# The 62 steps of each inversion of 32-blocks moved to GpSimd, and low parts of projection weights moved to VectorE

## The chip, the cores and the metric

One core of one Trainium2 chip runs the whole kernel. The metric is the device time of one execution in microseconds, taken as the median of several runs. The core has a matrix engine (TensorE, PE in the profile), VectorE (DVE), ScalarE (ACT), GpSimd (POOL) and SyncE (SP), each with its own list of instructions that it works through in order; they wait for each other through semaphores. DMA transfers are issued from the lists of SP and POOL.

## The reference, cut to what matters

The model has two layers. Layer 0 mixes tokens with a bidirectional gated delta rule, layer 1 with neighbourhood attention; each is followed by a gated feed-forward block with a convolution. There are 128 context tokens and 512 latent tokens of width 1024. The change lies in layer 0, in the triangular solve of the delta rule:

```
decay = jnp.where(lower, jnp.exp(jnp.where(lower, diff, 0.0)), 0.0)
kb = kc * bc[..., None]
a_mat = jnp.where(strict, jnp.einsum('nbhid,nbhjd->nbhij', kb, kc) * decay, 0.0)
eye = jnp.broadcast_to(jnp.eye(C, dtype=f32), a_mat.shape)
t_mat = lax.linalg.triangular_solve(eye + a_mat, eye, left_side=True, lower=True)
u = jnp.einsum('nbhij,nbhjd->nbhid', t_mat, vc * bc[..., None])
w = jnp.einsum('nbhij,nbhjd->nbhid', t_mat, kb * jnp.exp(gc)[..., None])
```

and in the projections that feed it (`proj = h @ w_in`), where queries, keys, values and gates of 8 heads of width 128 are made. The state is then carried over the chunks, in both directions, and the outputs are normalised and gated.

## The kernel before

**Products.** All large products are in float32 split in two: a high part, which the matrix engine takes at its faster rate, and a low part, the rest. `pass3` (L385, L386, L387) issues three matmuls for each: high times high, the data's low part times the weight's high, the data's high times the weight's low. `weights` (L359) issues the load of a 128x1024 block of weights on SP; `split` casts the high part on ScalarE (L373) and subtracts for the low part on `lo or net.lo_engine` (L375). In the stage of layer 0's mixer `net.lo_engine` is GpSimd; it is VectorE again from the output product's weights on, whose first two blocks (`go0` 0 and 1) are still split inside the stage.

**The mixer.** The class `Gdn` (L580) works head by head. A table written out by hand, `SCHED` (L573), gives the order in which the steps are put to the program: `k`, `q`, `v`, `z` are projections of one head (a product of 640 columns in two halves, a short convolution on VectorE at L442, an activation); `K` makes the decay masks (`decay`, L692 to L708), the token-wise keys, the five diagonal blocks of 128x128 in both directions (`keys`: PE at L761, then ten operations on VectorE into M at L786) and sends 32-blocks of them to a scratch tensor `md` (L795, DMAs on SP; a transpose on VectorE, L791, comes between). `I` inverts the unit triangular 32-blocks of two heads at once (`invert`), `M` puts four inverted 32-blocks together to one of 128 (`merge`, PE at L848 with copies on ScalarE and VectorE, L865 and L869 and L884), `Q` and `V` prepare queries and values, `S` is the scan over the blocks (`scan`, L906 to L972), `F` normalises and multiplies with the gate (`finish`, from L974), `a` is a tile of the modulation.

**The inversion.** Two heads give 80 partitions, each with one 32x32 block. `invert` loads lN from `md` (L806, on SP), sets lY to the unit matrix with two memsets on GpSimd (L808, L809), and runs 31 steps of two instructions: an outer product lP of a column of lN and a row of lY (L813), and its addition into lY (L819). The instructions have 31 to 256 elements per partition, and each needs the one before. Then lY goes to the scratch `yd` (L820, SP), a copy on VectorE writes its transpose over lN (L821), and that goes to `wd` (L822, SP). lN, lY and lP have one buffer each, so one inversion follows another. There are four: I0 to I3 for heads 0 and 1, 2 and 3, 4 and 5, 6 and 7.

**The merge** loads its blocks from `yd` and `wd` by DMAs on SP (L834 to L841) and first clears two corners of W6 (L829, L830) on GpSimd; W6 has one buffer.

**What sets the order.** The program is written in the order of `SCHED`, and a scheduler then puts the instructions of each engine in a list by readiness under its own costs and by priority. `PR` raises the priority of some steps: scans by 2000, inversions by 1000, merges by 500, keys by 200. Once made, the list of an engine is fixed: an instruction whose input is late holds up all that stand behind it on that engine.

Of the kernel before, what the change touches and what calls it, by code (L numbers as in the profile page):

```python
# [15 lines left out]
ALU = mybir.AluOpType  # L16
# [15 lines left out]
HBLK = ((0, 1, 2), (3, 4))  # L32
HN = 384
NFT = 22
PR = {"S": 2000, "I": 1000, "M": 500, "K": 200}
WSTB = 2
EARLY = 4
UNITS = 6
# [39 lines left out]
def run(steps):  # L78
    while True:
        try:  # L80
            next(steps)
        except StopIteration as end:
            return end.value
# [496 lines left out]
class Gdn:  # L580
# [218 lines left out]
    def invert(self, nh, md, yd, wd, name):  # L799

        nc = self.nc
        L = nh * 40
        N = self.gp.tile([128, 32, 32], F32, tag="lN", name=f"lN{name}", bufs=1)
        Y = self.gp.tile([128, 32, 32], F32, tag="lY", name=f"lY{name}", bufs=1)
        P = self.gp.tile([128, 256], F32, tag="lP", name=f"lP{name}", bufs=1)
        nc.sync.dma_start(N[:L], md.rearrange("h q d b r c -> (h q d b) r c")[:L])  # L806
        Yf = Y.rearrange("p r c -> p (r c)")
        nc.gpsimd.memset(Yf[:L], 0.0)  # L808
        nc.gpsimd.memset(Yf[:L, 0:1024:33], 1.0)  # L809
        for i in range(31, 0, -1):  # L810
            n = 32 - i
            pr = P[:L, : i * n].rearrange("p (j c) -> p j c", c=n)
            nc.vector.tensor_tensor(  # L813
                pr,
                N[:L, :i, i : i + 1].to_broadcast([L, i, n]),
                Y[:L, i : i + 1, i:].to_broadcast([L, i, n]),
                ALU.mult,
            )
            nc.vector.tensor_tensor(Y[:L, :i, i:], Y[:L, :i, i:], pr, ALU.add)  # L819
        nc.sync.dma_start(yd.rearrange("h q d b r c -> (h q d b) r c")[:L], Y[:L])  # L820
        nc.vector.tensor_copy(N[:L].rearrange("p r c -> p c r"), Y[:L])  # L821
        nc.sync.dma_start(wd.rearrange("h q d b r c -> (h q d b) r c")[:L], N[:L])  # L822
# [200 lines left out]
    def run(self):  # L1023
        net, nc, dp = self.net, self.nc, self.dp
        scr = {}
        adas = [(0, m, t) for t in range(KT) for m in (2, 4) if m == 2 or t < 4]

        def step(op, h):
            if op == "k":
                self.kT[h] = self.proj(1, h)  # L1030
            elif op == "q":
                self.qT[h] = self.proj(0, h)
            elif op == "v":
                self.vT[h] = self.proj(2, h)
            elif op == "K":
                if h % 2 == 0:
                    scr[h // 2] = [
                        dp.tile([2, 4, 2, NBLK, 32, 32], F32, tag=t, name=f"{t}{h // 2}", bufs=2)
                        for t in ("md", "yd", "wd")
                    ]  # L1040
                self.decay(h)
                self.keys(h, scr[h // 2][0][h % 2])
            elif op == "I":
                self.invert(2, *scr[h], h)
            elif op == "Q":
                self.queries(h)
            elif op == "V":
                self.values(h)
            elif op == "M":
                self.merge(h, scr[h // 2][1][h % 2], scr[h // 2][2][h % 2])  # L1050
            elif op == "S":
                self.scan(h)
            elif op == "F":
                self.finish(h)
            elif op == "z":
                self.gate(h)
            elif op == "a":
                for _ in range(min(h, len(adas))):
                    net.ada_tile(*adas.pop(0), self.gp, 1)

        for t in SCHED.split():
            if t[0] in PR:
                with net.tc.high_priority(PR[t[0]]):
                    step(t[0], int(t[1]))
            else:
                step(t[0], int(t[1]))
        while adas:
            net.ada_tile(*adas.pop(0), self.gp, 1)
        net.scale_vec(0, 2)
        self.first = {m: net.weights(net.a["w_gout"][m], KT, f"go0{m}") for m in range(2)}  # L1070
        for half in (0, 1):
            for h in range(8):
                for hf, c0, c1, _ in SEGS:
                    if hf == half:
                        g = self.G[h][:, c0:c1]
                        hh = net.hh[:, h, c0:c1]
                        nc.scalar.copy(hh, g)
                        nc.vector.tensor_tensor(net.hl[:, h, c0:c1], g, hh.bitcast(F32), ALU.subtract)
# [564 lines left out]
```

## Time and profile before

| what | value |
| --- | --- |
| median of 3 runs | 1931.02 us (1923.04 to 1935.49) |
| profiled execution | 1937.65 us |
| its span | 1935.7 us |
| mean granted clock of TensorE | 0.97 |
| first and last step of the four inversions | 116.1 to 156.4, 165.0 to 215.2, 323.9 to 378.3, 456.7 to 508.1 us |
| mixer of layer 0 | to about 595 us |

Times inside the trace count from the start of its span. Each row of the timeline gives start, duration, engine, line, operation, output and inputs by their names in the program, and shapes; what stands in brackets is the time in which the engine stood idle just before, and the operation that ended the wait. A line such as L813 is the line of the kernel before; lines behind 1042 are one higher in the changed kernel. PEld is TensorE's loading of weights, which goes on beside its matmuls. The granted clock is the share of full speed at which TensorE was let run.

### The profile page before, as it was taken

Reading aid. Unit: us, or ns where it says so; the run is one execution under the profiler, and the core shown is the slowest. Engines: PE = TensorE matmul, PEld = TensorE weight load, DVE = VectorE, ACT = ScalarE, POOL = GpSimd, SP = SyncE. Lnnn points to the kernel's source line nnn. Section 1 sums busy time; section 2 is a strip of 40 time slices with the busy share of each in tenths; the row PEclk is TensorE's granted clock in tenths of the full one; section 3 lists DMA queues with packets and bytes.
Section 4 is the critical chain, followed back from the end, with each engine's and each line's share of the span. In section 5 each row is a group of like instructions: output and inputs, shape, how many; then the busy total and the mean of one; then the engine's idle time right before and its main releaser. Section 6 shows DMA issues by size and latency. Waiting matters only on the chain.

```text
span 1935.7 us, 34324 instructions
## 1 busy us (share of the span) xinstructions
PE 1839.9 (95%) x13587; PEld 1749.1 (90%) x13587; DVE 1278.4 (66%) x3100; ACT 724.3 (37%) x1456; POOL 263.0 (14%) x317
## 2 busy tenths in 40 slices
PE   6889998999988999999999999999999999999998
PEld 5878888887878999999999988888889999999998
DVE  6687657757655999865356689655678843553564
ACT  4453344343334432133134344444454431331343
POOL 1332123121201211210000121111131000000000
PEclk9889899998888999999999999999999999999999
DMA  7223133222204355543223155322233322222231
GB/s 289 72 80 105 37 103 112 89 52 88 60 22 144 111 169 166 169 152 103 62 77 112 54 166 159 91 77 69 66 127 102 122 69 73 84 77 70 82 97 55
DMA packets 102480, 194.15 MB, mean 100 GB/s; under 512 B 39496, under 2 KB 59034, under 8 KB 99560
## 3 DMA queue, kind: packets, MB, share of 16 engines
q1 hardware_dynamic: 94528, 165.50, 27.7%
q0 software_dynamic: 7248, 25.94, 4.3%
q8 instruction: 107, 1.75, 0.4%
q14 instruction: 53, 0.43, 0.1%
q10 hardware_dynamic: 544, 0.52, 0.1%
HBM read 183.09 MB, written 12.46 MB: 101 GB/s over the span
## 4 chain that ended last, share of the span: by engine, by line
PE 46%; DVE 5%; issue 2%; DMA 2%; ACT 1%; POOL 0%; DVEq 0%; POOLq 0%; ACTq 0%
PE duv L385 4%; PE duv L386 4%; PE duv L387 4%; PE dug L385 4%; PE dug L386 4%; PE dug L387 4%; PE rdn L385 4%; PE rdn L387 4%; PE rdn L386 4%; DMA adr<-w_adar 1%; PE no L1323 1%; DMA bias<-cols 1%; PE dvn L385 1%; PE s L1269 1%; PE dvn L387 1%
## 5 line engine op out<-in xcount | busy, mean ns | idle before, releaser
L385 PE MATMUL duv<-hh,whuv 128*128 128x256 f32 (+1 forms) x704 | 216.7, 308 | 5.4 <-DVE yv L442 5.4
L385 PE MATMUL rdn<-F,whdn 128*128 128x384 f32 (+1 forms) x704 | 216.6, 308 | 3.5 <-DVE X L451 3.5
L386 PE MATMUL duv<-hl,whuv 128*128 128x256 f32 (+1 forms) x704 | 216.2, 307 | 0.0
L385 PE MATMUL dug<-hh,whug 128*128 128x256 f32 (+1 forms) x704 | 215.4, 306 | 0.8 <-DVE yg L442 0.8
L387 PE MATMUL duv<-hh,wluv 128*128 128x256 f32 (+1 forms) x704 | 216.0, 307 | 0.0
L386 PE MATMUL rdn<-F,whdn 128*128 128x384 f32 (+1 forms) x704 | 216.0, 307 | 0.0
L387 PE MATMUL rdn<-F,wldn 128*128 128x384 f32 (+1 forms) x704 | 215.8, 306 | 0.0
L386 PE MATMUL dug<-hl,whug 128*128 128x256 f32 (+1 forms) x704 | 215.4, 306 | 0.0
L387 PE MATMUL dug<-hh,wlug 128*128 128x256 f32 (+1 forms) x704 | 215.4, 306 | 0.0
L385 PEld LDWEIGHTS duv<-hh,whuv 128*128 128x128 f32 x704 | 132.8, 189 | 6.0 <-ACT whug L373 3.5
L385 PEld LDWEIGHTS rdn<-F,whdn 128*128 128x128 f32 x704 | 132.6, 188 | 4.2 <-issue 2.3
L385 PEld LDWEIGHTS dug<-hh,whug 128*128 128x128 f32 x704 | 132.2, 188 | 1.0 <-issue 1.0
L387 PEld LDWEIGHTS duv<-hh,wluv 128*128 128x128 f32 x704 | 132.8, 189 | 0.0
L386 PEld LDWEIGHTS rdn<-F,whdn 128*128 128x128 f32 x704 | 132.7, 189 | 0.0
L387 PEld LDWEIGHTS rdn<-F,wldn 128*128 128x128 f32 x704 | 132.7, 189 | 0.0
L386 PEld LDWEIGHTS duv<-hl,whuv 128*128 128x128 f32 x704 | 132.6, 188 | 0.0
L387 PEld LDWEIGHTS dug<-hh,wlug 128*128 128x128 f32 x704 | 132.2, 188 | 0.0
L386 PEld LDWEIGHTS dug<-hl,whug 128*128 128x128 f32 x704 | 132.2, 188 | 0.0
L451 DVE SCALAR_TENSOR_TENSOR X<-rdn,mods,X 128x128 f32<-128x128 f32 (+1 forms) x144 | 54.9, 433 | 116.5 <-PE rdn L387 116.4
L373 ACT CAST whdn<-wstdn 128x896 fp32r<-128x896 f32 (+1 forms) x48 | 47.0, 979 | 214.1 <-PE rdn L386 122.0
L373 ACT CAST whug<-wstug 128x1024 fp32r<-128x1024 f32 x44 | 46.2, 1050 | 137.7 <-PE dug L386 114.5
L375 DVE TENSOR_TENSOR wldn<-wstdn,whdn 128x896 fp32r<-128x896 f32 (+1 forms) x48 | 54.3, 1132 | 60.6 <-ACT whdn L373 60.5
(701 smaller groups left out, 4909.3 us busy)
## 6 DMA issues: line engine op xcount, KB each, us to landing
wstuv<-w_up SPq DMA_DIRECT2D x44, 512.0 KB, 3.5
wstug<-w_up SPq DMA_DIRECT2D x44, 512.0 KB, 3.5
adat<-w_ada SPq DMA_DIRECT2D x20, 1024.0 KB, 5.7
adr<-w_adar POOLq DMA_DIRECT2D x80, 256.0 KB, 3.2
wstdn<-w_dn SPq DMA_DIRECT2D x32, 448.0 KB, 3.4
wstdn<-w_dn SPq DMA_DIRECT2D x16, 512.0 KB, 3.6
adr<-w_adar SPq DMA_DIRECT2D x32, 256.0 KB, 2.9
wstqT<-w_gin SPq DMA_DIRECT2D x8, 512.0 KB, 3.6
```

Of the source, the lines that this page charges most:

```text
L373: nc.scalar.copy(wh[:, c], st[:, c])
L375: ins = eng.tensor_tensor(wl[:, c], st[:, c], wh[:, c].bitcast(F32), ALU.subtract).ins
L385: nc.tensor.matmul(out, a, mh, start=first, stop=False)
L386: nc.tensor.matmul(out, a, ml, start=False, stop=False)
L387: ins = nc.tensor.matmul(out, b, mh, start=False, stop=last).ins
L451: nc.vector.scalar_tensor_tensor(x, ps[:, base + c0 : base + c1], self.mod(l, gi, m, v), x, ALU.mult, ALU.add)
L1269: nc.tensor.matmul(ss[e][:, o], qb[H[e]], kk[H[e]], start=True, stop=True, tile_position=(64 * e, 0))
L1323: nc.tensor.matmul(out, vw[:n, cb, j, H[e]], pt[:n, 2 * e + j], start=(j == 0), stop=False, tile_position=(0, 64 * e))
```

## The change

Three edits. Both instructions of a step of the inversion (L813, L819) are issued on GpSimd in place of VectorE; the load, the memsets, the final copy (L821) and the DMAs stay where they were. The added priority of the inversions goes from 1000 to 100. And once the first inversion has been put to the program, `net.lo_engine` is VectorE, so that low parts of weights that come behind it in `SCHED` are subtracted there.

```diff
-PR = {"S": 2000, "I": 1000, "M": 500, "K": 200}
+PR = {"S": 2000, "I": 100, "M": 500, "K": 200}
...
         for i in range(31, 0, -1):
             n = 32 - i
             pr = P[:L, : i * n].rearrange("p (j c) -> p j c", c=n)
-            nc.vector.tensor_tensor(
+            nc.gpsimd.tensor_tensor(
                 pr,
                 N[:L, :i, i : i + 1].to_broadcast([L, i, n]),
                 Y[:L, i : i + 1, i:].to_broadcast([L, i, n]),
                 ALU.mult,
             )
-            nc.vector.tensor_tensor(Y[:L, :i, i:], Y[:L, :i, i:], pr, ALU.add)
+            nc.gpsimd.tensor_tensor(Y[:L, :i, i:], Y[:L, :i, i:], pr, ALU.add)
...
             elif op == "I":
                 self.invert(2, *scr[h], h)
+                net.lo_engine = nc.vector
```

In the lists of the changed kernel 28 low parts of 128x1024 stand on VectorE that stood on GpSimd: of v0, q1, v2, the gates and all later projections, 26 in all, and of the first two output blocks. Those of k2, q0, k3 and v1 stay on GpSimd. Rows of the lists follow; a row gives line, operation, output and inputs (with buffer numbers), and shape.

VectorE before, while head 3's blocks M3 are made and the first inversion runs:

```order
L819 TENSOR_TENSOR lY0_1325<-lY0_1325,lP0_1326 80x8x24
L786 SCALAR_TENSOR_TENSOR M3_1303<-kk3p_1297,D3_1289,dec3_1244 128x128
L813 TENSOR_TENSOR lP0_1326<-lN0_1324,lY0_1325 80x175
L786 SCALAR_TENSOR_TENSOR M3_1303<-kk3s_1296,D3_1289,dec3_1244 128x128
L819 TENSOR_TENSOR lY0_1325<-lY0_1325,lP0_1326 80x7x25
```

VectorE in the change, at the same place (wlzs0 and wlzs1 are low parts of gate weights, D3 the factors of head 3):

```order
L375 TENSOR_TENSOR wlzs0_2415<-wstzs00_2412,whzs0_2414 128x1024
L442 SCALAR_TENSOR_TENSOR qT1_1642<-dqT11_1617,sm_61,qT1_1642 128x256
L821 COPY lN0_1324<-lY0_1325 80x32x32
L375 TENSOR_TENSOR wlzs1_2474<-wstzs10_2471,whzs1_2473 128x1024
L752 TENSOR_SCALAR k3ss_1278<-k3ss_1278 128x5
L775 RECIPROCAL rk23_1287<-k3ss_1278 128x5
L779 TENSOR_TENSOR D3_1289<-rk23_1287,beta_669 128x5 x2
L780 TENSOR_SCALAR D3_1289<-D3_1289 128x5
L781 TENSOR_TENSOR D3_1289<-D3_1289,edl_691 128x5
L780 TENSOR_SCALAR D3_1289<-D3_1289 128x5
L781 TENSOR_TENSOR D3_1289<-D3_1289,edl_691 128x5
L786 SCALAR_TENSOR_TENSOR M3_1303<-kk3p_1297,D3_1289,dec3_1244 128x128
```

The copy that ends the inversion, which stood behind M3 and the last step, now stands ahead of all of head 3's D and M.

VectorE in the change, in the scan of head 3 (vm, S and w are the scan's values of one block; dec4 belongs to head 4's queries):

```order
L929 TENSOR_SCALAR vm301_4042<-sb301_4035,D3_1289 128x128
L929 TENSOR_SCALAR vm314_4057<-sb314_4050,D3_1289 128x128
L821 COPY lN2_3608<-lY2_3609 80x32x32
L966 SCALAR_TENSOR_TENSOR S030_4047<-S03_4006,egl_690,sb301_4035 128x128
L898 TENSOR_TENSOR dec4_2810<-kq4s_3693,dec4_2810 128x512
L966 SCALAR_TENSOR_TENSOR S130_4062<-S13_4008,egl_690,sb314_4050 128x128
```

The copy of the third inversion stands between two operations of the scan. In the same way that of the second stands in head 1's scan, between the operations w and vm, and that of the fourth in head 5's, behind the first two vm.

SP in the change, where the second inversion's load stands (W61 is head 1's corner tile, adat021 a block of modulation weights, ns00 and ns01 head 0's final states):

```order
L836 DMA W61_2001<-wd0_720 32x5x32
L837 DMA W61_2001<-wd0_720 32x5x32
L838 DMA W61_2001<-yd0_719 32x5x32
L839 DMA W61_2001<-yd0_719 32x5x32
L795 DMA md1_1013<-MT3_1314 32x5x32 x4
L172 DMA adat021_2364<-w_ada 128x2048
L940 DMA out_state<-ns00_1861 128x128
L940 DMA out_state<-ns01_1871 128x128
L806 DMA lN1_1515<-md1_1013 80x1024
```

Before, the load of lN1 stood ahead of head 1's merge loads and of both out_state. On POOL the 62 steps of an inversion stand mostly in one piece; for the fourth they stand behind the memsets of W66 (head 6's corner tile):

```order
L829 MEMSET W66_5370 32x5x32
L830 MEMSET W66_5370 32x5x32
L989 TENSOR_TENSOR so4_5260<-so4_5260,mhalf_70 128x5
L813 TENSOR_TENSOR lP3_5042<-lN3_5040,lY3_5041 80x31
L819 TENSOR_TENSOR lY3_5041<-lY3_5041,lP3_5042 80x31
```

In the list of before no step of an inversion stands on POOL at all.

## The prediction

> **What bounds the kernel now.** I read the page's first part first (span 1935.7 us), then the windows over the four stretches in which an inversion runs, then the groups of VectorE, PE's waits, and the timeline where the order changes.
>
> ```profile
> PE 1839.9 (95%) x13587; PEld 1749.1 (90%) x13587; DVE 1278.4 (66%) x3100; ACT 724.3 (37%) x1456; POOL 263.0 (14%) x317
> ```
>
> PE is busy for 95% of the span, so nothing is gained by relieving another engine except where PE itself stands or runs below full clock. The windows (length; busy time and count of PE, PEld, DVE, ACT, POOL; granted clock; DMA) show where that is: the four inversion stretches, and the rest from 595 us on.
>
> ```profile
> 116.00:157.00 41.00, 33.32 (x221) 29.90 (x220) 39.05 (x126) 15.07 (x40) 11.52 (x7) 0.88 0.28 86
> 165.00:217.00 52.00, 47.01 (x495) 42.16 (x494) 39.78 (x118) 16.68 (x57) 5.61 (x6) 0.90 0.22 60
> 324.00:379.00 55.00, 53.28 (x468) 47.50 (x469) 44.32 (x129) 17.40 (x51) 7.54 (x5) 0.94 0.27 91
> 457.00:508.00 51.00, 47.73 (x332) 43.89 (x325) 42.91 (x126) 19.47 (x64) 9.38 (x4) 0.94 0.16 48
> 595.00:1935.00 1340.00, 1314.27 (x9288) 1277.58 (x9287) 871.58 (x1906) 484.27 (x799) 136.18 (x216) 0.99 0.33 103
> ```
>
> From 595 us on PE is 98% busy at clock 0.99, and the change touches nothing there. In the four stretches VectorE is nearly full, 39.05 us of 41 in the first, and PE loses something. The groups of VectorE from 100 to 595 us say what fills it:
>
> ```profile
> L813 DVE TENSOR_TENSOR lP<-lN,lY 80x31 f32<-80x31 f32 (+15 forms) x124 | 51.0, 411 | 7.8 <-DMA lN<-md 6.4
> L819 DVE TENSOR_TENSOR lY<-lY,lP 80x31 f32<-80x31 f32 (+15 forms) x124 | 49.3, 398 | 1.4
> ```
>
> The 248 steps take 100.3 us of VectorE, 25.1 us per inversion, spread over 40 to 54 us each because other work of VectorE stands between them. PE's waits between 100 and 640 us (total, times, longest) are short. The one that returns below is for VectorE's reads of two banks into M:
>
> ```profile
> PE gb L692 <- DVE M L786: 3.9, 3, 1.9
> ```
>
> **The gain, bounded.** All 248 steps leave VectorE; the order of the change shows that, so "it does not do what it says" is no rival. In return VectorE gets 28 low parts, the two of the first output weights among them.
>
> ```profile
> L375 DVE TENSOR_TENSOR wluv<-wstuv,whuv x42: 1207/1224/1227, 657.6 to 1855.9; 128x1024 fp32r<-128x1024 f32 x42
> ```
>
> ```profile
> L375 DVE TENSOR_TENSOR wldn<-wstdn,whdn 128x896 fp32r<-128x896 f32 (+1 forms) x48 | 54.3, 1132 | 60.6 <-ACT whdn L373 60.5
> ```
>
> That is 28 x 1.224 = 34 us of work, so VectorE is relieved by 100.3 - 34 = 66 us. A low part also waits at the head of VectorE for ScalarE's cast of the high part: 60.6 / 48 = 1.26 us each in the second row, 35 us for 28; even with those VectorE gains 31 us. What PE can win is bounded by its own losses in the four stretches: it stood 41 - 33.32 + 52 - 47.01 + 55 - 53.28 + 51 - 47.73 = 17.7 us, and the clock cost 33.32 x 0.12 + 47.01 x 0.10 + 53.28 x 0.06 + 47.73 x 0.06 = 14.8 us. The relief lies between 0 and **32 us**. I take all of it, because each stall found below lets all other work catch up behind it.
>
> **The price of an inversion on GpSimd (T).** No GpSimd row of before has this form; the nearest are its two-input operations and a pair of memsets.
>
> ```profile
> L375 POOL TENSOR_TENSOR wlzs<-wstzs,whzs x8: 2341/2394/3419, 128.6 to 503.3; 128x1024 fp32r<-128x1024 f32 x8
> L375 POOL TENSOR_TENSOR wlno<-stg,whno x8: 1291/1514/1762, 1421.5 to 1433.4; 128x512 fp32r<-128x512 f32 x8
> ```
>
> ```profile
> L1179 POOL TENSOR_TENSOR bias<-bias,mask x64: 499/614/1486, 1118.2 to 1396.0; 128x248 f32<-128x248 f32 x32, 128x184 f32<-128x184 f32 x16, 128x192 f32<-128x192 f32 x16
> ```
>
> ```profile
> 180.46 0.22 POOL L829 MEMSET W<- 32x160 f32 x1 [16.61 <-PE p L848]
> 180.73 0.23 POOL L830 MEMSET W<- 32x160 f32 x1
> ```
>
> ```profile
> 118.46 1.17 POOL L773 TENSOR_TENSOR irk<-k2ss,half 128x5 f32<-128x5 f32 x1 [5.73 <-DVE k2ss L752]
> ```
>
> One inversion is 62 dependent instructions with 2 x 5456 = 10,912 elements per partition (i times 32 - i summed over 31 steps, twice), 176 on average. From 1024 and 512 elements: (2.341 - 1.291) / 512 = 2.05 ns per element and 0.24 us fixed, so 10,912 x 2.05 ns + 62 x 0.24 = 37.3 us. From 1024 elements and the shortest bias operation (184 elements): (2.341 - 0.499) / 840 = 2.19 ns and 0.096 us, 29.9 us. The memsets stand 0.05 us apart, so 62 x 0.05 = 3.1 us between instructions: T = 33 to 40 us. (The first two fences are the form of a low part; then the bias, the memsets, a power.) Other GpSimd work falls between the steps, a power of 1.17 us and two decay masks per head, some 3 us per inversion: 33 to 43. I take **T = 40**, from the middle of the slopes plus these. The lowest bound is the memset, 160 elements with nothing read: 62 x 0.27 = 17 us. The highest is the slowest 512-element row, 1.762 us for 2.9 times the mean size: 62 x 1.762 x 176 / 512 + 62 x 0.24 = 52 us.
>
> By these rows a two-input operation of 128x1024 is 2394 / 1224 = 1.96 times as long on GpSimd as on VectorE. The Trainium skill (GPSIMD Engine Reference, section 4.1, Engine selection) speaks against the change: elementwise work belongs on VectorE, GpSimd being about twice as slow with two inputs. The trace agrees for this size; doubling the 25.1 us would give T = 50 and, by the sum worked out below, 2013 us.
>
> **Where the wait goes.** In the order of before the copy L821 stands behind the steps on the same engine and waits for nobody. In that of the change it stands on VectorE ahead of head 3's M for the first inversion, and inside the scans of heads 1, 3 and 5 for the others; it waits for GpSimd's last step, and VectorE runs its list in order. So VectorE stands at the copy, PE behind VectorE. I counted PE's work between marked matmuls along both orders, at the spacing at which they start in the trace (148.94 to 149.11 here, 0.17 us), and scaled by what the same stretch took before.
>
> ```profile
> 101.56 1.16 PE L761 MATMUL kk1s<-kT 128*128 128x128 f32 x8
> ...
> 148.94 0.33 PE L387 MATMUL dzs<-hh,wlzs 128*128 128x384 f32 x1
> 148.95 0.35 DVE L786 SCALAR_TENSOR_TENSOR M<-kk3s,D,dec 128x128 f32<-128x128 f32 x1
> 149.11 0.34 PE L385 MATMUL dzs<-hh,whzs 128*128 128x384 f32 x1
> ...
> 149.32 2.45 POOL L375 TENSOR_TENSOR wlzs<-wstzs,whzs 128x1024 fp32r<-128x1024 f32 x1 [5.27 <-ACT whzs L373]
> ...
> 149.71 2.22 DVE L813 TENSOR_TENSOR lP<-lN,lY 80x135 f32<-80x135 f32 x1
> ...
> 169.04 0.50 PE L848 MATMUL p<-W,M 32*32 32x32 f32 x10
> ...
> 189.09 0.34 SPq L940 DMA_DIRECT2D out_state<-ns  x1
> ...
> 220.76 0.61 DVE L953 SCALAR_TENSOR_TENSOR w<-sb,negc,virk 128x128 f32<-128x128 f32 x2 [0.45 <-PE sb L951]
> ```
>
> First inversion: the steps begin at 116.1 us as before and end at 156; the copy 1.1 (a row of it stands below), a low part 1.2, nine small operations of 0.16 and ten of head 3's M at 0.35 make 164 with their gaps. The next group of transposes, q0ts, needs banks that M frees. From kk1s to q0ts PE has 37 us of work, plus some 3 of waits: it is there at 142. Stall **22 us**.
>
> Second: on SP the load of lN1 now stands behind the merge loads of heads 0 and 1 and head 0's two out_state, 189.09 - 169.04 = 20 us after head 0's merge; with the landing time below the steps start at 24.5, end at 64.5, and the copy at 65.6. VectorE's w operations just ahead of the copy came 220.76 - 169.04 = 51.7 after the merge; PE's work up to there falls from 36.5 to 34.4 us, so 48. Stall **18**.
>
> ```profile
> L821 DVE COPY lN<-lY x4: 1077/1116/1128, 156.6 to 508.1; 80x1024 f32<-80x1024 f32 x4
> ```
>
> ```profile
> L806 SPq DMA_DIRECT2D lN<-md x4: 314/319/378, 112.1 to 443.8; - x4
> ...
> DMA to landing us min/median/max: 3.5/4.4/6.8
> ```
>
> ```profile
> 305.38 1.16 PE L761 MATMUL kk5s<-kT 128*128 128x128 f32 x8
> ...
> 316.13 0.31 SPq L806 DMA_DIRECT2D lN<-md  x1
> ...
> 349.43 0.35 DVE L929 TENSOR_SCALAR vm<-sb,D 128x128 f32<-128x128 f32 x1 [0.61 <-PE sb L925]
> ...
> 428.93 1.48 PE L761 MATMUL kk7s<-kT 128*128 128x128 f32 x6
> ...
> 450.51 0.79 PE L848 MATMUL p<-W,M 64*64 64x64 f32 x10 [2.12 <-DVE W L869]
> ...
> 466.94 0.61 DVE L929 TENSOR_SCALAR vm<-sp,D 128x128 f32<-128x128 f32 x2 [0.46 <-PE sp L925]
> ```
>
> Third: the load goes out 316.13 - 305.38 = 10.8 us after kk5s and lands 4.4 later; steps from 15 to 55, copy (1.1) done at 56. VectorE was past head 3's vm 44 us after kk5s; by the same counting, with the steps gone, it stands there at 40. Stall **16**. Fourth: on GpSimd the memset of head 6's W6 stands ahead of the steps and waits for head 5's merge, 450.51 - 428.93 = 21.6 us after kk7s; steps from 22 to 62, copy 63. VectorE passes head 5's vm at 38 in before; PE's order puts 34 us of work ahead of it where 25 stood, so 45. Stall **18**.
>
> The stalls sum to 74 at T = 40, and each follows T one for one, so the net is 74 + 4 x (T - 40) - 32 = **4T - 118 us**: nothing at T = 29.5, +42 at 40. The profiled execution, 1937.65 us, becomes 1980; the shown median, 1931.02, is 0.9966 of the profiled time, so **1973 us**. The likeliest case's own range goes from T = 35 with the whole relief (+22, 1953) to T = 43 with half of it (4 x 43 - 86 - 16 = +70, 2001).
>
> The moved low parts are late for PE in no row of before, and leaving GpSimd frees 28 x 2.39 = 67 us there; I cost them at nothing beyond VectorE's time. If ScalarE's casts arrive late, the 1.26 us each eat the relief.
>
> The Trainium skill (TensorE: Matmul & The Clock Gate, Part 1) lets PE's clock fall to half after an idle window of about 3.4 us; four restarts at half clock would be an estimate of +7 us by that page. No row here shows it alone.
>
> **Rivals.** *A, the relief decides* (faster). GpSimd needs no more than 25 us, or the work ahead of the copy on VectorE is that much longer, and VectorE never stands. For: the memset's 0.27 us per instruction, and VectorE needs 23 to 26 us from the start of the steps to its copy in each of the four places above. Against: every two-input row is above 0.499 us. At T = 24, 4 x 24 - 118 = -22: **1909**. *B, a wash*: T of 25 to 34, stalls and relief cancel; T = 30 gives +2, **1933**. For: the bias rows with T = 33. Against: the interruptions. *C, much slower*: GpSimd and VectorE shut each other out where both read two operands from SBUF. The step at 149.71, beside GpSimd's at 149.32, took 2.22 us, where L813's mean is 0.411, and ended only after GpSimd's operation had. With 62 GpSimd operations in a row, VectorE's low parts and scans would hold them up in turn; at T = 50 the net is +82, 2020 of the profiled execution, **2013**. It decides from T = 45. Against: in the scans VectorE reads one operand from PSUM. The Trainium skill (SBUF — State Buffer, SBUF: two separate sides) calls the pair of ports that the two share an exclusive lock held for the whole instruction; the pair of rows agrees.
>
> **Chances.** The main forecast 0.52, C 0.13, B 0.17, A 0.18. A measurement of this kernel tells about 1% (19 us) from no change, so faster by over 1% is A, 0.18; within 1% is B, 0.17; slower is the main case and C, 0.65. The range reaches from A's 1909 to just beyond C's 2013: 1909 to 2017, leaving half of A and half of C out.
>
> **What would show it.** Right: L821 on VectorE with an idle time of 10 us or more ahead of it, released by GpSimd's L819, four times; PE idle behind it; POOL busy near 263 - 67 + 4 x 37 = 344 us and VectorE near 1278 - 66 = 1212; 35 us or more from first to last step. Wrong: L821 with no wait on GpSimd (A); steps under 0.5 us each (B); VectorE operations stretched to several times their length beside the steps (C).

## The result, and the profile after

| | median | runs | ratio to before (95% interval) |
| --- | --- | --- | --- |
| before | 1930.29 us | 7 (1923.04 to 1939.76) | |
| the change | 1943.05 us | 7 (1937.91 to 1950.03) | 1.0065 (1.004 to 1.009) |

The change is slower by 12.8 us, where 42 were forecast: a difference that can be measured, but within the 1% that the prediction called no change. The profiled execution took 1937.91 us, the fastest of the seven, while that of before (1937.65) was among the slower of its own; so the two traces end at the same time, and a net of 12.8 us has to be read from the medians.

The head of the page after:

```profile
span 1936.2 us, 34305 instructions
...
PE 1811.8 (94%) x13587; PEld 1728.7 (89%) x13587; DVE 1209.2 (62%) x2880; ACT 724.8 (37%) x1458; POOL 328.5 (17%) x537
```

VectorE lost 69 us of work, GpSimd gained 65. The steps, now groups of POOL (the groups from 100 to 600 us; busy time and mean ns of one, idle time before):

```profile
L819 POOL TENSOR_TENSOR lY<-lY,lP 80x31 f32<-80x31 f32 (+15 forms) x124 | 67.6, 545 | 9.6
L813 POOL TENSOR_TENSOR lP<-lN,lY 80x31 f32<-80x31 f32 (+15 forms) x124 | 67.1, 541 | 26.7 <-DMA lN<-md 17.4
```

From first to last step the four inversions take 41.3, 39.6, 38.3 and 38.9 us (the first starts at 114.6 us and ends at 155.9). PE's waits between 100 and 640 us, which before held nothing longer than 4.3 us, now begin with four long ones and a shorter fifth (total, times, longest):

```profile
PE adp L194 <- DVE adev L189: 20.4, 3, 19.5
PE kk3s L761 <- ACT k3ts L751: 17.0, 1, 17.0
PE sb L950 <- DVE S L966: 15.7, 2, 15.0
PE sb L925 <- ACT osb L957: 12.3, 1, 12.3
PE adp L184 <- DVE M L786: 3.6, 1, 3.6
```

The longest wait of each of the first four rows is one stall, and the four sum to 63.8 us. The waits of VectorE and ScalarE in the same stretch lead on to GpSimd:

```profile
DVE lN L821 <- POOL lY L819: 65.7, 4, 25.7
DVE osb L991 <- POOL so L989: 25.2, 8, 12.9
```

```profile
ACT dec L708 <- POOL dec L703: 17.3, 1, 17.3
```

The timeline shows which of them stand behind which stall (start, duration, engine; in brackets the idle time before and what ended it). First inversion:

```profile
144.90 1.45 POOL L703 TENSOR_SCALAR_AFFINE_SELECT dec<-dec 128x640 f32<-128x640 f32 x2
146.32 0.61 POOL L819 TENSOR_TENSOR lY<-lY,lP 80x220 f32<-80x220 f32 x1
146.38 1.27 ACT L708 ACTIVATE dec<-dec 128x1280 f32<-128x1280 f32 x1 [17.28 <-POOL dec L703]
```

Head 3's masks stand on GpSimd between the steps, come late there, and ScalarE's exponential of them waits 17.28 us; the squares that kk3s needs stand behind it on ScalarE. So this stall is not made by the copy, although VectorE waits 25.7 us at it too; what the copy adds here is PE's 3.6 us for head 3's M, right behind it. Second inversion:

```profile
221.71 1.17 POOL L989 TENSOR_TENSOR so<-so,mhalf 128x5 f32<-128x5 f32 x1
```

```profile
222.91 1.66 DVE L991 TENSOR_SCALAR osb<-osb,so 128x128 f32<-128x128 f32 x5 [12.93 <-POOL so L989]
224.49 0.60 DVE L953 SCALAR_TENSOR_TENSOR w<-sb,negc,virk 128x128 f32<-128x128 f32 x2
```

A power of head 0's normalisation is queued behind steps on GpSimd; head 1's scan stands behind it on VectorE. Of the four, only the third and fourth are the copy's:

```profile
362.81 1.03 DVE L821 COPY lN<-lY 80x1024 f32<-80x1024 f32 x1 [15.62 <-POOL lY L819]
...
364.06 0.79 PE L950 MATMUL sb<-S,kT 128*128 128x128 f32 x2 [15.01 <-DVE S L966]
```

```profile
492.47 1.03 DVE L821 COPY lN<-lY 80x1024 f32<-80x1024 f32 x1 [21.28 <-POOL lY L819]
...
494.20 1.01 PE L194 MATMUL adp<-sel,adev 128*128 128x2 f32 x4 [19.46 <-DVE adev L189]
```

PE stands 64 us, and the kernel loses 13. The rest was won back elsewhere, and not in the four stretches alone. Two stretches between and behind the inversions, before and then after (length; PE, PEld, DVE, ACT, POOL; clock):

```profile
380.00:460.00 80.00, 72.39 (x671) 64.08 (x670) 44.44 (x143) 30.19 (x87) 21.53 (x19) 0.91 0.29 76
510.00:600.00 90.00, 75.93 (x615) 66.61 (x615) 47.97 (x133) 35.36 (x115) 8.21 (x7) 0.79 0.25 76
```

```profile
380.00:460.00 80.00, 79.54 (x774) 73.82 (x773) 49.76 (x148) 35.13 (x90) 13.87 (x26) 0.98 0.32 95
510.00:600.00 90.00, 86.11 (x778) 78.84 (x777) 56.76 (x163) 43.34 (x145) 4.66 (x6) 0.96 0.23 72
```

In these two PE stood 7.6 + 14.1 us before and 0.5 + 3.9 after, and the clock cost 6.5 + 15.9 before and 1.6 + 3.4 after: 35 us outside the four stretches. Not all of it need be relief, since work that was held up at the stalls fills these stretches too.

### The profile page after: what moved, and what is told of

It reads as the page before. It is cut to its first block, busy times and chain, and to the rows that moved or that the text cites. A ratio compares the mean times of both kernels' runs of the same rounds, so it can differ in the third digit from the quotient of the medians.

```text
span 1936.2 us, 34305 instructions
## 1 busy us (share of the span) xinstructions
PE 1811.8 (94%) x13587; PEld 1728.7 (89%) x13587; DVE 1209.2 (62%) x2880; ACT 724.8 (37%) x1458; POOL 328.5 (17%) x537
## 4 chain that ended last, share of the span: by engine, by line
PE 49%; DVE 4%; issue 2%; DMA 1%; ACT 1%; POOL 0%; DVEq 0%; POOLq 0%; ACTq 0%
PE duv L385 4%; PE duv L387 4%; PE duv L386 4%; PE dug L385 4%; PE dug L387 4%; PE dug L386 4%; PE rdn L385 4%; PE rdn L387 4%; PE rdn L386 4%; PE dvn L385 1%; PE dqn L385 1%; PE dvn L386 1%; PE dvn L387 1%; PE no L1324 1%; PE s L1270 1%
```

## The experiments

Every ratio below is to the kernel before on the same chip, with its 95% interval. Theory S and theory R were set up first, to tell the price of the stalls from the size of the relief; L and Q came after the first four runs.

**The three edits apart.** The steps without the low parts (the change without `net.lo_engine = nc.vector` behind `invert`):

```diff
                 self.invert(2, *scr[h], h)
-                net.lo_engine = nc.vector
```

> The change without its third edit: the 62 steps on GpSimd, low parts of weights left on GpSimd all through the mixer. VectorE has 34 us less to do than in the change; five low parts of 2.4 us stand between steps of the inversions on GpSimd. Theory S (a microsecond taken from VectorE in the mixer is worth about 0.8 us, 51 for 66): 26 us more relief, 12 us longer inversions, 1929 us, between 1920 and 1940. Theory R (relief is exhausted at 32 us, and low parts on GpSimd lengthen the inversions on the path): 12 to 20 us slower than the change, 1955 to 1963 us.

Measured 1960.57 us, 1.0155 (1.0138 to 1.0171), +30 us: R's number, not S's. The low parts without the steps:

```diff
 (the kernel before)
                 self.invert(2, *scr[h], h)
+                net.lo_engine = nc.vector
```

> The kernel before with the third edit alone: steps of the inversion on VectorE, the 28 low parts on VectorE as well, 34 us more of work there. Theory S (0.8 us per microsecond of VectorE's work in the mixer): 1930 + 27 = 1957 us, between 1947 and 1967. Theory R (only the four stretches count, in which some 12 of the 28 low parts fall): 1930 + 14 = 1944 us or less, between 1930 and 1946.

Measured 1914.79 us, 0.9922 (0.9898 to 0.9946): 16 us faster than before, where both theories had it slower. Giving VectorE 34 us of work made the kernel faster. The two add up: -15.7 + 30.0 = +14.3, and the change has +12.8. The second edit, the priority of 100, was not run alone: with 1000 in its place the lists of VectorE and ScalarE are the same row for row, and on PE, GpSimd and SP 9, 15 and 2 rows change places.

So the change is a gain and a larger loss, and the gain is in the edit that I had costed at nothing. The steps' groups on VectorE in low_parts_alone show where it is from; before they read 51.0 and 49.3 us:

```profile
L813 DVE TENSOR_TENSOR lP<-lN,lY 80x31 f32<-80x31 f32 (+15 forms) x124 | 41.2, 332 | 1.8 <-DMA lN<-md 0.8
L819 DVE TENSOR_TENSOR lY<-lY,lP 80x31 f32<-80x31 f32 (+15 forms) x124 | 41.1, 332 | 1.1
...
L991 DVE TENSOR_SCALAR osb<-osb,so 128x128 f32<-128x128 f32 x40 | 9.8, 280 | 6.1 <-POOL so L989 6.1
...
L780 DVE TENSOR_SCALAR D<-D 128x5 f32<-128x5 f32 x16 | 2.5, 163 | 0.0
```

```profile
L991 DVE TENSOR_SCALAR osb<-osb,so 128x128 f32<-128x128 f32 x40 | 15.7, 427 | 10.3 <-POOL so L989 10.3
...
L780 DVE TENSOR_SCALAR D<-D 128x5 f32<-128x5 f32 x16 | 6.9, 438 | 0.0
```

The first fence is low_parts_alone, the second the kernel before. The same instructions are shorter by 18.0 + 5.9 + 4.4 us. In the kernel before, those that were stretched began while a low part ran on GpSimd, and ended with it or up to 0.28 us behind it, as at 306.84 us:

```profile
306.84 2.38 DVE L780 TENSOR_SCALAR D<-D 128x5 f32<-128x5 f32 x1
```

```profile
306.76 2.44 POOL L375 TENSOR_TENSOR wlkT<-wstkT,whkT 128x1024 fp32r<-128x1024 f32 x1
```

Counting every VectorE operation between 60 and 600 us that lasted over 0.25 us longer than the shortest of its form gives 20 of them, all beside a low part on GpSimd, 36.7 us in all; in low_parts_alone there is none. VectorE's busy time is nearly the same in both (1278.4 and 1272.9 us): 34 us of low parts came, 37 us of standing went. Theory L says that this is the gain; theory Q that the low parts come sooner, or that GpSimd's list is free.

**Theory L tested.** The low parts stay on GpSimd, in four instructions each:

```diff
-        ins = eng.tensor_tensor(wl[:, c], st[:, c], wh[:, c].bitcast(F32), ALU.subtract).ins
+        for i in range(4) if lo is None and eng is nc.gpsimd else (None,):
+            q = c if i is None else slice(i * 256, i * 256 + 256)
+            ins = eng.tensor_tensor(wl[:, q], st[:, q], wh[:, q].bitcast(F32), ALU.subtract).ins
```

> The kernel before with each low part on GpSimd split into four instructions of 128x256 (in the mixer; some 0.62 us each, 2.5 us together, like the one of 2.39): no work changes its engine and no low part comes sooner. Theory L (the third edit wins because a GpSimd instruction holds VectorE's operations with two SBUF inputs for its whole length): the stretching of VectorE's operations falls from 36.7 us to 8 to 15 us, and half or more of the 16 us is won, 1919 us, between 1914 and 1924. Theory Q (it wins because low parts come sooner on VectorE or because GpSimd's list is free): 1930 us, between 1926 and 1936.

Measured 1914.69 us, 0.9918 (0.9892 to 0.9945): all of the gain with no work on another engine. A quarter takes 0.736 us, so GpSimd works longer than before, and the stretching by the same count is 17.0 us, more than L expected, in 39 pieces. The steps' means fall from 411 and 398 ns to 373 and 375. Since the first quarter also lands sooner, the order was turned round:

```diff
-        for i in range(4) if lo is None and eng is nc.gpsimd else (None,):
+        for i in (3, 2, 1, 0) if lo is None and eng is nc.gpsimd else (None,):
```

> As low_parts_in_quarters, but the four instructions of a low part are issued from the last quarter to the first, so that the quarter that PE needs first comes last, when the undivided low part would have come, or later. Theory L (short instructions on GpSimd hold VectorE for less): still 1915 us, between 1911 and 1920. Theory Q (the quarters win because the first quarter lands 1.7 us sooner): 1930 us, between 1925 and 1936.

Measured 1919.98 us, 0.995 (0.9933 to 0.9968), on the edge of L's range: 10 of the 16 us stay with the first quarter last, at 18.5 us of stretching. The two intervals touch, so whether the other 5 us are the sooner landing is left open; most of the gain goes with the shorter hold. One rival no run excludes: the scheduler makes the lists anew for every edit. Of VectorE's 2923 instructions other than low parts, 41 stand in another order in low_parts_in_quarters than in the kernel before, and 227 in low_parts_alone, so some of the gain may be the order's.

Then the hold was to be brought back without moving anything, by idle work on GpSimd beside the low parts on VectorE (`x` is a slice of the high part):

```diff
 (low_parts_alone)
+        if lo is None and self.replay is not None:
+            for i in (0, 256, 512):
+                x = wh[:, i : i + 256].bitcast(F32)
+                nc.gpsimd.tensor_tensor(self.replay, x, x, ALU.subtract)
```

> Steps and the 28 low parts on VectorE, as in low_parts_alone; added on GpSimd, for each of those low parts, three subtractions of 128x256 with two inputs from SBUF into a scratch tile that nobody reads, together about 2.3 us, released by the same cast on ScalarE. Theory L (in the kernel before, a low part on GpSimd holds VectorE's operations of two SBUF inputs: 20 operations stretched by 36.7 us in all between 60 and 600 us; that is what the move of the low parts wins): the stretching returns, 25 us or more of it, and most of the 16 us with it, 1928 us, between 1922 and 1938. Theory Q (the move wins because low parts come sooner, or take less room): nothing of that is undone here, 1915 us, between 1910 and 1920.

Measured 1913.55 us, 0.9935 (0.9915 to 0.9955). Q's number came and L's did not, but L's premise was not met either: the stretching that came back was 10.9 us in 29 pieces of some 0.4 us, not 25 us in pieces of 2. It is inconclusive on long holds, and shows that short ones cost nothing here. With copies in place of the subtractions (`nc.gpsimd.tensor_copy(self.replay, x)`, four of them):

> The same with four copies of 128x256 (one input from SBUF) in place of the three subtractions, some 2 us of GpSimd per low part. Theory L with the hold bound to two inputs on both sides: VectorE is not stretched, 1915 us, between 1910 and 1920. If any GpSimd operation that reads SBUF holds VectorE: like idle_two_inputs, 1926 us or so. If GpSimd's own list being busy is what costs (its masks and powers come late): both kernels at 1920 to 1930 without any stretched operation.

Measured 1914.31 us, 0.9928 (0.9905 to 0.9951), with 0.3 us of stretching by the same count. That count leaves out pieces of less than 0.25 us. From 0.1 us up there are 21 pieces here, 20 of them beside a copy, of some 0.2 us each and 4.3 us in all, where low_parts_alone has 0.2 us: a copy with one input, 0.40 us long, holds VectorE too, only briefly, and L's form with two inputs on both sides does not stand. Some 63 us of added work in GpSimd's list do no harm, against that part of Q. One long instruction of 128x1024 beside the low parts was not run, so long holds were never brought back. Low parts on VectorE from the start of the mixer (`net.lo_engine = nc.vector` where it was GpSimd):

> The kernel before with one edit: low parts on VectorE from the start of the mixer, so the four of k2, q0, k3 and v1 too; steps on VectorE. Theory L: in low_parts_alone no VectorE operation is stretched any more, so nothing is left to win; 4 x 1.22 = 5 us more of VectorE's work, half of it on the path: 1917 us, between 1912 and 1921. Theory Q: each moved low part wins 16 / 28 = 0.6 us, 1912 us, between 1908 and 1915.

Measured 1913.82 us, 0.9931 (0.9907 to 0.9955): a microsecond from low_parts_alone and inside both ranges, so it tells L and Q not apart; there is nothing more to win.

**The price of the steps.** First the relief without the stalls:

```diff
-        for i in range(31, 0, -1):
+        for i in range(1, 0, -1):
```

> The change with 1 of the 31 steps of each inversion; the other 30 are left out, so it computes other blocks. Nothing is left on GpSimd that VectorE could wait for, and VectorE has its 66 us less: this measures the relief without any stall. Theory S: the relief is 50 to 64 us, 1930 - 57 = 1873 us, between 1862 and 1882. Theory R: it is at most the 32 us of the prediction, 1898 us or more.

Measured 1866.64 us, 0.9664 (0.9643 to 0.9685): 64 us, twice the bound of the prediction. This run also takes away the inversions' own length (0.6 us each in place of some 40 to 54), so the 64 us hold what that is worth besides the relief. PE's longest wait there between 100 and 570 us is 1.6 us. Theory R's 32 us do not fit; what R said of steps_alone came true although the relief is not exhausted: PE's stalls there last 16.0, 7.8, 14.1, 17.4 and 20.5 us, 75.8 in all, which leaves 46 us of relief behind the +30. Next, inversions made longer:

```diff
+            for _ in range(8 if i == 1 else 0):
+                nc.gpsimd.tensor_tensor(P[:L, :5], self.half[:L], self.half[:L], ALU.pow)
```

> The change with eight powers of 80x5 (1.17 us each in the trace, results overwritten) put on GpSimd ahead of the last step of each inversion, so that each inversion lasts 9.4 us longer while the other lists stay nearly as they are. By the prediction's sum each stall follows the inversion one for one: 4 x 9.4 = 38 us, 1981 us, between 1972 and 1988. Rival (part of each stall is made up behind it, or two of the four stalls belong to masks and powers that stand on GpSimd ahead of these last steps): 15 to 28 us, 1958 to 1971 us.

Measured 1985.78 us, 1.0274 (1.0238 to 1.0311), 42.7 us over the change. The inversions last 51.2, 49.3, 48.2 and 48.8 us, 39.4 us more in sum: one for one in total, as the prediction's sum had it. VectorE's wait at the copy (L823 there) grows from 65.7 to 101.5 us:

```profile
DVE lN L823 <- POOL lY L821: 101.5, 4, 34.9
```

The growth stands at the four copies alone. PE's waits:

```profile
PE adp L194 <- DVE adev L189: 30.2, 2, 29.8
PE sb L952 <- DVE S L968: 25.9, 2, 25.3
PE sb L927 <- ACT osb L959: 23.8, 2, 13.9
PE kk3s L761 <- ACT k3ts L751: 16.0, 1, 16.0
PE adp L184 <- DVE M L786: 14.0, 2, 13.8
```

The masks' stall (16.0 us) and the power's (13.9) hardly move. The third and fourth stall grow by some 10 us each, the wait for M behind the first copy from 3.6 to 13.8 us, and the second copy makes a stall of its own, 9.9 us.

Last, who waits. The copy L821 on GpSimd:

```diff
-        nc.vector.tensor_copy(N[:L].rearrange("p r c -> p c r"), Y[:L])
+        nc.gpsimd.tensor_copy(N[:L].rearrange("p r c -> p c r"), Y[:L])
```

> The change with one more edit: the copy L821 that ends each inversion is issued on GpSimd, so nothing on VectorE waits for GpSimd's last step. Lists of VectorE and PE are else almost those of the change. Theory S (PE's 64 us of standing in the profile of the change is the price of the copy's place on VectorE, and the relief of VectorE is worth 50 us or more over the whole mixer): the waits of VectorE for L819, 65.7 us, are gone, PE's four stalls of 12 to 20 us shrink to the waits of the merges for their data, 5 to 8 us each; 1943 - 35 = 1908 us, between 1895 and 1918. Theory R (the relief is only the 32 us that I allowed, and a stall costs less than it lasts since PE catches up behind it): the stalls were two thirds absorbed, so taking them away gives back some 20 us; 1923 us, between 1918 and 1932.

Measured 1925.81 us, 0.9964 (0.9943 to 0.9984): 17 us better than the change, half of what S expected and in R's range. Its waits of PE say why:

```profile
PE adp L184 <- DMA adat<-w_ada: 17.6, 2, 17.1
PE kk3s L761 <- ACT k3ts L751: 16.0, 1, 16.0
PE sb L925 <- ACT osb L957: 11.4, 1, 11.4
```

The fourth stall is gone. The first two stay, since masks and power still stand behind steps. The third comes back by another list: SP waits for the last step at L820, and a load of modulation weights stands behind it.

```profile
SPq L820 <- POOL lY L819: 18.9, 1, 18.9
```

```profile
362.15 0.33 SPq L820 DMA_DIRECT2D yd<-lY  x1
364.13 0.32 SPq L822 DMA_DIRECT2D wd<-lN  x1
364.55 0.37 SPq L172 DMA_DIRECT2D adat<-w_ada  x1
```

So the two stores went to GpSimd as well (`nc.gpsimd.dma_start` for yd and wd):

> The kernel copy_on_gpsimd with the two stores L820 and L822 (yd, wd) issued on GpSimd behind its last step and copy, in place of SP, so that nothing on SP waits for GpSimd's steps. In copy_on_gpsimd PE stood 17.1 us at a modulation tile whose load stood on SP behind L820 of the third inversion. Theory S' (what counts is which list waits for GpSimd's last step): that stall goes, and 3 us go to GpSimd's issuing of DMAs: 1926 - 14 = 1912 us, between 1904 and 1918. Rival: the wait turns up at the merge of heads 4 and 5 or elsewhere, 1922 to 1930 us.

Measured 1917.34 us, 0.995 (0.9935 to 0.9964). The stall at the modulation tile is gone, and two are left, 15.4 and 10.9 us, the masks' and the power's. For these:

```diff
-        nc.sync.dma_start(N[:L], md.rearrange("h q d b r c -> (h q d b) r c")[:L])
+        nc.gpsimd.dma_start(N[:L], md.rearrange("h q d b r c -> (h q d b) r c")[:L])
...
-        W6 = self.gp.tile([128, NBLK, 64], F32, tag="W6", name=f"W6{h}", bufs=1)
+        W6 = self.gp.tile([128, NBLK, 64], F32, tag="W6", name=f"W6{h}", bufs=2)
...
-                self.decay(h)
+                if h != 3:
+                    self.decay(h)
+                if h == 2:
+                    self.decay(3)
```

> The kernel copy_and_stores_on_gpsimd with three more edits: head 3's decay masks are made along with head 2's, so that they do not stand behind steps of the first inversion on GpSimd; the load of lN is issued on GpSimd, not behind merge loads on SP; W6 has two buffers, so that its memsets do not wait for the merge just before. In copy_and_stores_on_gpsimd PE stood 15.4 us for ScalarE's exponential of head 3's masks and 10.9 us behind the power of head 0's normalisation, both late on GpSimd behind steps. Theory S' (these two are what is left of the price of the steps): 1917 - 15 - 7 = 1895 us, between 1888 and 1904, the fastest so far. Rival (the merges then wait for the inversion itself, some 39 us long in any case): 1908 to 1917 us.

Measured 1918.57 us, 0.9946 (0.9924 to 0.9968): no faster than the kernel that it starts from, as the rival had it, though 1.6 us above the rival's range. Its waits of PE:

```profile
PE p L848 <- DMA W<-wd: 26.8, 2, 24.3
PE sb L925 <- ACT osb L957: 12.0, 1, 12.0
```

The masks hold nobody up any more, and PE runs on to head 0's merge and stands there 24.3 us for the first inversion itself. The second inversion still began at 191.3 us behind a memset of W6, so the power stayed late: that half of the edit did not do what it was for.

## Why the prediction was wrong, point by point

- **T = 40: right.** 41.3, 39.6, 38.3 and 38.9 us were measured; 541 and 545 ns per instruction stand between the two ways of pricing (482 and 602 ns on average).
- **The stalls: the size nearly, the place half.** 74 us forecast, 63.8 found, by stall 17.0, 12.3, 15.0, 19.5 for 22, 18, 16, 18. I put all four on the copy L821. The first belongs to head 3's masks and the second to head 0's power, both on GpSimd behind steps. I had seen this work in GpSimd's list and counted it only as 3 us that lengthen the inversion, not as work that is itself held up and waited for. At the first inversion the copy cost PE only 3.6 us more behind the masks' 17.0.
- **One for one with T: right in sum.** 39.4 us more of inversion gave 42.7 us, all of it at the four copies; the masks' and the power's stalls did not follow.
- **The relief of 0 to 32 us: the step that failed.** "What PE can win is bounded by its own losses in the four stretches." In the change 63.8 - 12.8 = 51 us must have come back by the medians (63 between the two profiled executions, which end 0.5 us apart), and one_step measured 64 us. The bound left out PE's losses in the rest of the mixer. The windows from 60 us to the mixer's end, for the kernel before, the change and one_step, show them:

```profile
60.00:595.00 535.00, 481.05 (x3962) 434.52 (x3962) 367.53 (x1093) 214.45 (x607) 110.51 (x83) 0.91 0.26 77
60.00:598.00 538.00, 455.60 (x3958) 416.22 (x3957) 298.22 (x872) 214.56 (x608) 176.62 (x303) 0.91 0.26 76
60.00:521.00 461.00, 445.48 (x3962) 405.52 (x3962) 295.79 (x871) 215.34 (x610) 44.22 (x63) 0.98 0.30 89
```

Reckoned as in the prediction, PE stood 54 us before and the clock cost 43: 97 us, three times what the four stretches hold. In one_step 15.5 and 8.9 us of that are left. In the change PE stands 82.4 us, of which only 18.6 lie outside the four stalls. What held PE up between the stretches before was not followed wait by wait; part of it goes with VectorE's standing beside low parts, which is the next point.

- **The low parts "at nothing beyond VectorE's time": wrong.** They won 16 us. I had the two rows at 149.32 and 149.71 us on the table and used them only for what GpSimd might do to VectorE after the change (rival C); they showed what it was already doing before. The step's 100.3 us on VectorE held 18 us of this standing, so even its price was not a price of the work.
- **The rivals.** The time fell into B's band, near its 1933, but not by B's cause: T was not 25 to 34. C did not decide: the steps are short, and operations of VectorE were stretched by 2.5 us in all in the change. In the other direction six of GpSimd's 248 step instructions lasted 1.4 to 1.7 us beside a low part on VectorE, 5.5 us too long in all. A's cause is nowhere.
- **What the profile was to show.** POOL 328.5 us for 344 and VectorE 1209.2 for 1212: right. L821 with over 10 us of idle time came three times, not four; at the second VectorE had already lost its time to the power, and waited some 3 us.
- **The half clock behind a stall** shows now: behind the first stall PE's granted clock is 0.50 for 3.5 us, which is part of the stalls' price that the measured net already holds. This agrees with the Trainium skill (TensorE: Matmul & The Clock Gate, Part 1), by which the clock is at half after an idle window of about 3.4 us.

```profile
151.90:155.40 3.50, 3.46 (x13) 3.47 (x14) 0.00 (x0) 0.00 (x0) 2.87 (x9) 0.50 0.00 0
```

The sum with the measured terms: 63.8 us of stalls less 51 of relief. Of the 29 us by which the forecast of 42 was off, 19 are the relief's and 10 the stalls'. Of the 51, low_parts_alone accounts for 16, and by subtraction the steps' leaving for 35; in steps_alone, 75.8 us of stalls for 30 lost leave 46 for it. The two splits overlap: 18 us of the standing beside low parts was the steps' own, and goes with either edit. No run shows the steps leaving VectorE with neither stall nor change of latency.

## What to carry to other kernels

Before costing an instruction that moves, ask whether its duration in the trace is its own: where the same form has 0.35 us here and 2.2 us there, look at what the neighbouring engine was doing, and count what goes away with that neighbour as a gain. When dependent work moves to another engine, which also works through its list in order, look up everything else in that engine's list and who waits for it; a result that is late there stops engines that never touch the moved work, and taking away one waiter passes the wait to the next list. The kernel that the experiments point to leaves the steps on VectorE and only moves or shortens the low parts: 1914 to 1915 us, 0.992 of before, and by the medians 0.985 of the change.

## What the runs showed of the hardware

- The 20 operations of VectorE that a low part on GpSimd held had their operands in SBUF alone, and they need not have two inputs: a TENSOR_SCALAR of 128x5 took 2.38 us in place of 0.16. The 40 or so with an operand in PSUM that began inside a low part all ran at their own length, such as M at 149.44 us within GpSimd's 149.32 to 151.77:

```profile
149.44 0.35 DVE L786 SCALAR_TENSOR_TENSOR M<-kk3s,D,dec 128x128 f32<-128x128 f32 x1
```

- It seems to go by which of the two comes first. Of the operations in SBUF alone that began inside a low part, a microsecond or more before its end, 18 were held and 6 were not. Five of the six stand one behind the other in a single low part, from 503.42 us on; that low part took 3.42 us in place of some 2.39, and the next operation of VectorE was held until it ended. The sixth is a transpose (L791, at 435.10 us); why it ran freely is open.

```profile
503.30 3.42 POOL L375 TENSOR_TENSOR wlzs<-wstzs,whzs 128x1024 fp32r<-128x1024 f32 x1 [3.62 <-ACT whzs L373]
504.50 2.33 DVE L813 TENSOR_TENSOR lP<-lN,lY 80x87 f32<-80x87 f32 x1
```

- Short holds are nearly free here: with 10.9 to 18.5 us of them in pieces of about 0.4 us the kernel took 0 to 5 us more than low_parts_alone, where 36.7 us in pieces of 2 went with 16.
- One-input copies on GpSimd (0.40 us for 128x256) held VectorE as well, for some 0.2 us at a time and 4.3 us in all.
